# One plain chunk instead of two in each feed-forward block, and a pair opened among its matmuls

## The chip, the cores and the metric

The kernel runs on one core of a Trainium2 chip. The metric is the device time of one execution in microseconds (us), as the median of several runs. TensorE multiplies, VectorE and ScalarE work elementwise, GpSimd (POOL) does a few elementwise rows and issues the transfers that add to what is in SBUF, SyncE (SP) issues the loads.

## The reference

A trunk of two layers over two batches (512 and 256 tokens, width 1024). Each layer is `x += 1/2 SwiGLU(RMSNorm(x)); x += Mixer(RMSNorm(x)); x += 1/2 SwiGLU(RMSNorm(x))`, the mixers being a gated linear recurrence (layer 0) and windowed attention (layer 1). So there are four feed-forward blocks, here f0 to f3:

```python
def swiglu_ffn(x, w1, w2):               # w1: 1024 x 5632, w2: 2816 x 1024
    gate, up = jnp.split(x @ w1, 2, axis=-1)
    return (jax.nn.silu(gate) * up) @ w2
```

## The kernel before

**Split numbers.** Every operand is kept as a high half (a cast, on ScalarE) and a low half (what the cast left, a subtraction on VectorE), and a product is three matmuls: high by high, high by low, low by high. `split` does this for activations (L355 and L356), `quad_steps` for weights (L217 and L218).

**Seven products for eight.** The 768 tokens are two halves of 384, the 1024 inputs are two parts, and a chunk of 128 hidden units has a gate and an up column block. A *pair* (`up_pair`, matmuls on L549) makes the 2 x 2 x 2 blocks of one chunk by seven products p1 to p7 (Strassen's scheme in Winograd's form), each of four input tiles by three matmuls: 84 matmuls of 128x384. Each product has a weight factor (a11, a12, a21, a22 or sums of them) and an activation factor, by `FACTOR`: p1 takes b00 and p2 takes b10 (both of the first token half), p3 takes b11, and p7, p5, p6, p4 take the sums t3, t1, t2, t4 of all four blocks b00, b10, b01, b11. (In bRC, R is the input part and C the token half.) `sums` makes these four with subtractions and splits them.

**Plain chunks.** The sums need the second token half, which is normalised and transposed (`turn`, L421, L432) only while the block starts. So each block begins with `PLAIN` = 2 chunks without the scheme (`up_plain`, matmuls L350 to L352): 48 matmuls for a token half, 96 for a chunk. The other 20 chunks are pairs; after each four, `down_quad` multiplies by w2 in the same way.

**Weights.** `plan_ffn` lists the loads; `load_next` issues them on SP's queue into four raw buffers (`wr`), `take` and `ahead` stage their splits into eight buffers (`w`). For a pair, a partial tile `s` (L203) and a21 get their sums by transfers that add (`into`, L151, on POOL's queue). Two more sums, a11 += a21 ("second") and a12 += a11 ("fourth"), are additions on VectorE (L224), placed behind p5's and p4's split. p6 uses the first, p3 the second. p5's low half is made on POOL.

**Order.** A scheduler sets the order on each engine when the program is built, from the order in which the code is written; each engine then works through its own list in order. `later` and `run_later` put the second half's normalisation, transposes and sums between the plain chunks' matmuls.

Of the kernel before, what the change touches and what calls it, by code (L numbers as in the profile page):

```python
# [16 lines left out]
P = 128  # L17
D = 1024
DFF = 2816
NC = D // P  # L20
# [13 lines left out]
SEQS = ((0, TA), (TA, TB))  # L34
H = T // 2
HB = H // P
PLAIN = 2
GROUPS = (NF - PLAIN) // 4
WBUFS = 8
RAWBUFS = 4  # L40
# [14 lines left out]
class Trunk:  # L55
# [97 lines left out]
    def load_next(self):  # L153
        key, srcs, shape, how = self.queue.pop(0)
        if how in (TOK, OUT):
            self.loaded.append((len(srcs), self.tok_steps(key, srcs, how), 4))
            return
        raws = []
        for src in srcs:
            t = self.wp.tile([P, 1024], F32, tag="wr", name=self.name("wr"), bufs=RAWBUFS)  # L160
            raw = t[:, : shape[0] * shape[1]].rearrange("p (a b) -> p a b", a=shape[0])
            if len(srcs) < 4:
                src = src.rearrange("(k p) c -> p k c", p=P)
            self.last_load = self.nc.sync.dma_start(raw, src)
# [5 lines left out]
        free = 4  # L170
        if self.more.get(key):
            tail = self.tail_steps(key, self.more[key], how)
            steps = [step for both in zip(steps, tail) for step in both]
            free = 8
        self.loaded.append((len(raws), steps, free))

    def wtile(self):
        return self.wp.tile([P, 1024], F32R, tag="w", name=self.name("w"), bufs=WBUFS)
# [11 lines left out]
    def quad_steps(self, key, raws, srcs, order):  # L190
        nc = self.nc
        flat = lambda t: t.rearrange("p a b -> p (a b)")
        up = len(raws) == 2
        if up:
            a11, a12, a21, a22 = (flat(t[:, h : h + 4, :]) for t in raws for h in (0, 4))
            three = [srcs[1].rearrange("(k p) c -> p k c", p=P)[:, :4, :]]
        else:
            a11, a12, a21, a22 = (flat(t) for t in raws)
            three = [srcs[2][:, i : i + 1, :] for i in range(2)]
        s3 = []  # L200
        for i, src in enumerate(three):
            t = self.wp.tile([P, 512], F32, tag="s3", name=self.name("s3"), bufs=2)
            self.last_load = nc.sync.dma_start(t.rearrange("p (a b) -> p a b", a=src.shape[1]), src)  # L203
            self.into(t, a11[:, i * 512 : (i + 1) * 512])
            s3.append(t)
        self.into(a21, a22)

        def split(name, srcs, eng=None):
            if up:
                w = self.wtile()  # L210
                hi, lo = w[:, :512], w[:, 512:]
            else:
                hi, lo = self.wtile(), self.wtile()
            n = srcs[0].shape[-1]
            for i, src in enumerate(srcs):
                h, l = (t[:, i * n : (i + 1) * n] for t in (hi, lo))
                nc.scalar.copy(h, src)  # L217
                (eng or nc.vector).tensor_sub(l, src, h.bitcast(F32))  # L218
# [89 lines left out]
    def stage_next(self):  # L308
        if not self.loaded:
            self.load_next()  # L310
        steps = self.loaded[0][1]
        n, go = steps.pop(0)
        go()
        self.held += n
        if not steps:
            self.loaded.pop(0)
        inuse = lambda e: e[0] if len(e[1]) > e[2] or e[0] < 4 else 0
# [15 lines left out]
    def ahead(self):  # L333
        while self.queue or self.loaded:
            if not self.loaded:
                self.load_next()
            if self.held + self.loaded[0][1][0][0] > WBUFS:
                return
            self.stage_next()

# [132 lines left out]
        put("t2", b11)  # L473

    def sums(self):
        for kp in range(2):
            tiles = (self.tn[(i // 2, i % 2)][:, kp] for i in range(4))
            self.mix(*tiles, lambda name, src: self.put(name, kp, src))

    def spill_factors(self):  # L480
        self.kept = {}
# [22 lines left out]
            self.later(self.sums)  # L504

    def plan_ffn(self, tag, w1, w2):
        def up(i):
            gate, up = (w1[:, c * P : (c + 1) * P] for c in (i, NF + i))
            if i < PLAIN:
                self.plan((tag, i, 0), gate, (NC, P))  # L510
                self.plan((tag, i, 1), up, (NC, P))
            else:
                self.plan_quad((tag, i), (gate, up), (NC, P), UP)
# [12 lines left out]
    def up_plain(self, tag, j, half):  # L526
        pss = []
        for c in range(2):
            wh, wl = self.take((tag, j, c))
            ps = self.ps(H)  # L530
            for k in range(NC):
                b = self.operand(f"b{k // 4}{half}", k % 4)
                self.mm3(ps, (wh[:, k, :], wl[:, k, :]), b, k == 0, k == NC - 1)
                if half == 0 and k in (((), (2, 6)), ((3, 7), (3, 7)))[j][c]:
                    self.run_later()
            if half:
                self.done((tag, j, c))
            pss.append(ps)
        t = self.tmp(H)
# [19 lines left out]
    def up_pair(self, tag, j, opened=None):  # L559
# [29 lines left out]
        self.last_act = nc.scalar.activation(v, v, AF.Silu).ins  # L589
        self.last_dve = nc.vector.tensor_mul(w, v, w).ins  # L590
        yield w
        self.ahead()

    def down_quad(self, tag, g, hid):
# [82 lines left out]
    def ffn(self, tag, next_row):  # L677
        for g in range(GROUPS):
# [7 lines left out]
            def gather(ts, kp):  # L686
                self.mix(ts[0], ts[1], ts[2], ts[3], lambda name, src: put(name, src, kp))

            if g == 0:
                ts = {}  # L690
                for half in range(2):
                    for j in range(PLAIN):
                        t = ts[2 * j + half] = self.up_plain(tag, j, half)
                        name = f"b{j}{half}"
                        if name != "b01":
                            put(name, t, 0)
                gather(ts, 0)
                self.run_later(len(self.deferred))
            for kp in range(2):
                if g == 0 and kp == 0:  # L700
                    continue
                ts = []
                for j in range(2):
                    for half, t in enumerate(self.up_pair(tag, 4 * g + 2 * kp + j)):
                        ts.append(t)
# [925 lines left out]
```

## Time and profile before

| | |
|---|---|
| median of 3 runs | 2758.43 us (2758.16 to 2761.84) |
| profiled execution | 2759.27 us, span 2757.5 us |
| TensorE busy | 2736.1 us (99%) |
| VectorE busy | 2201.0 us (80%) |
| ScalarE busy | 1396.5 us (51%) |
| GpSimd busy | 460.7 us (17%) |
| granted TensorE clock | 0.999 |

In a row of a timeline the first number is the start in us from the span's start, the second how long the merged rows take from first start to last end, then engine, line, operation, what is written from what, shape and count; in brackets the idle time ahead and what ended it. In a row of groups the number behind the bar is the busy time, then the mean of one in ns. In a row of transfers the last number is the time from issue to landing. Matmuls overlap, so their starts tell more than their durations.

### The profile page before, as it was taken

What the parts mean: (1) busy time and instruction counts of PE and PEld (TensorE: products, weight loads), DVE (VectorE), ACT (ScalarE), POOL (GpSimd) and SP (SyncE); (2) the same over time, 40 slices, a digit from 0 to 9 for tenths busy, and PEclk for the clock granted to TensorE, in tenths of its full rate; (3) what the DMA queues carried; (4) which work ended last, traced back from release to release, by engine and by line L of the source; (5) the groups of instructions that cost most, each with busy time, mean ns of one, the idle gap of its engine ahead of it and who ended that gap; (6) DMA issues with size and microseconds to landing.
All of it is one profiled execution on the core that took longest, in us unless ns stands there. A gap on an engine that the chain in (4) does not pass through costs nothing. (4 is left out here: it accounts for less than half of the span.)

```text
span 2757.5 us, 40950 instructions
## 1 busy us (share of the span) xinstructions
PE 2736.1 (99%) x15081; PEld 2547.1 (92%) x15081; DVE 2201.0 (80%) x3766; ACT 1396.5 (51%) x2621; POOL 460.7 (17%) x507
## 2 busy tenths in 40 slices
PE   8999999999999999999999999999999999999998
PEld 8999999989999889999998999999888889999997
DVE  8788788767887888788878887887847868788877
ACT  6344444634455675444455543444458855444453
POOL 2111121200000101211120121112005611211120
PEclk9999999999999999999999999999999999999999
DMA  6554556751122743555454355545424422655453
GB/s 171 132 122 116 126 140 167 217 153 39 39 60 65 201 121 82 145 134 127 114 138 126 77 145 128 126 118 142 130 77 112 89 69 73 146 134 128 116 135 111
DMA packets 355048, 330.46 MB, mean 120 GB/s; under 512 B 14664, under 2 KB 271648, under 8 KB 354848
## 3 DMA queue, kind: packets, MB, share of 16 engines
q1 hardware_dynamic: 303744, 225.61, 27.6%
q0 software_dynamic: 46800, 88.76, 18.3%
q10 hardware_dynamic: 4304, 13.49, 1.4%
q8 instruction: 118, 1.93, 0.3%
q14 instruction: 82, 0.67, 0.1%
HBM read 226.87 MB, written 15.73 MB: 88 GB/s over the span
## 5 line engine op out<-in xcount | busy, mean ns | idle before, releaser
L549 PE MATMUL ps<-big,w 128*128 128x384 f32 x6720 | 1168.5, 334 | 0.0
L549 PEld LDWEIGHTS ps<-big,w 128*128 128x128 f32 x6720 | 1165.7, 188 | 1.4
L217 ACT CAST w<-wr 128x512 fp32r<-128x512 f32 x600 | 417.2, 706 | 651.6 <-PE ps L549 300.1
L218 DVE TENSOR_TENSOR w<-wr,w 128x512 fp32r<-128x512 f32 (+1 forms) x520 | 436.1, 842 | 138.1 <-ACT w L217 122.3
L615 PE MATMUL ps<-w,big 128*128 128x512 f32 x2016 | 460.7, 389 | 0.0
L615 PEld LDWEIGHTS ps<-w,big 128*128 128x128 f32 x2016 | 377.9, 188 | 78.8 <-DVE x L675 0.6
L151 POOL DMA_DIRECT2D s<-wr x126 | 110.5, 884 | 1220.7 <-DMA s<-in_ffn_w_dram 324.7
L675 DVE SCALAR_TENSOR_TENSOR x<-ps,x 128x512 f32<-128x512 f32 x420 | 272.7, 684 | 13.7 <-PE ps L647 13.1
L350 PE MATMUL ps<-big,w 128*128 128x384 f32 x640 | 219.2, 344 | 1.5 <-ACT w L184 1.0
L351 PE MATMUL ps<-big,w 128*128 128x384 f32 x640 | 215.1, 336 | 0.4 <-DVE big L356 0.3
L352 PE MATMUL ps<-big,w 128*128 128x384 f32 x640 | 214.5, 335 | 0.0
L355 ACT CAST big<-tA 128x384 fp32r<-128x384 f32 x308 | 153.6, 513 | 101.6 <-DVE tA L583 34.2
L356 DVE TENSOR_TENSOR big<-tA,big 128x384 fp32r<-128x384 f32 x308 | 176.3, 585 | 5.3 <-ACT big L355 3.4
L151 POOL DMA_DIRECT2D wr<-wr x109 | 95.3, 874 | 510.2 <-DMA wr<-in_ffn_w_dram 175.1
L831 PE MATMUL ps<-w,big 128*128 128x512 f32 x756 | 177.1, 392 | 0.1
L647 PE MATMUL ps<-w,big 128*128 128x512 f32 x756 | 174.5, 391 | 0.7 <-DVE x L675 0.6
L647 PEld LDWEIGHTS ps<-w,big 128*128 128x128 f32 x756 | 141.3, 188 | 30.5 <-DVE x L675 1.5
L831 PEld LDWEIGHTS ps<-w,big 128*128 128x128 f32 x756 | 140.5, 188 | 29.2 <-DVE w L356 0.6
L218 POOL TENSOR_TENSOR w<-wr,w 128x512 fp32r<-128x512 f32 x80 | 130.4, 1630 | 169.7 <-ACT w L217 152.6
L224 DVE TENSOR_TENSOR wr<-wr,wr 128x512 f32<-128x512 f32 (+1 forms) x120 | 123.6, 1030 | 20.4 <-issue 20.2
L350 PEld LDWEIGHTS ps<-big,w 128*128 128x128 f32 x640 | 120.1, 188 | 2.5 <-ACT w L184 1.3
L351 PEld LDWEIGHTS ps<-big,w 128*128 128x128 f32 x640 | 120.4, 188 | 1.4 <-DVE big L356 1.2
(219 smaller groups left out, 3647.3 us busy)
## 6 DMA issues: line engine op xcount, KB each, us to landing
wr<-in_ffn_w_dram SPq DMA_DIRECT2D x256, 512.0 KB, 4.0
s<-wr POOLq DMA_DIRECT2D x126, 256.0 KB, 4.5
s<-in_ffn_w_dram SPq DMA_DIRECT2D x120, 256.0 KB, 3.2
wr<-wr POOLq DMA_DIRECT2D x80, 256.0 KB, 3.9
wr<-in_hg_w_in_dram SPq DMA_DIRECT2D x32, 512.0 KB, 3.9
wr<-wr POOLq DMA_DIRECT2D x29, 512.0 KB, 4.6
spill<-x ACTq DMA_DIRECT2D x12, 512.0 KB, 3.9
kept<-big POOLq DMA_DIRECT2D x8, 768.0 KB, 7.9
```

Source lines behind the costliest of these rows:

```text
L151: self.nc.gpsimd.dma_start(out, src, accum_op=ALU.add)
L217: nc.scalar.copy(h, src)
L218: (eng or nc.vector).tensor_sub(l, src, h.bitcast(F32))
L350: nc.tensor.matmul(out, a[0], b[0], start=first, stop=False)
L351: nc.tensor.matmul(out, a[0], b[1], start=False, stop=False)
L352: nc.tensor.matmul(out, a[1], b[0], start=False, stop=last)
L356: self.nc.vector.tensor_sub(lo, src, hi.bitcast(F32))
L549: self.nc.tensor.matmul(ps, a[x], b[y], start=first and k == 0 and i == 0, stop=k == 3 and i == 2, skip_group_check=True,)
L615: nc.tensor.matmul(ps, a[x], w[y], start=name == chain and kp == 0 and q == 0, stop=kp == 1 and q == 2, skip_group_check=True,)
L647: nc.tensor.matmul(ps, a[x], w[y], start=name == chain and k == 0 and q == 0, stop=k == 2 and q == 2, skip_group_check=True,)
L675: self.nc.vector.scalar_tensor_tensor(x, ps, c, x, ALU.mult, ALU.add)
L831: nc.tensor.matmul(ps, x[:, sl], y, start=fresh and k == 0 and q == 0, stop=k == 3 and q == 2, skip_group_check=True,)
```

## The change

`PLAIN` becomes 1. Chunk 1 is a pair of a new form, `opened_pair`, whose p1 and p2 stand among the plain chunk's matmuls for the first token half (they need only b00 and b10). The rest of it follows the plain chunk's second token half, in the order p3, p7, p5, p6, p4. p3 gets a bank of its own. For this pair alone (`OPEN`) the "second" and "fourth" weight sums are made by adding transfers, behind p1's and p2's split, so p3's weight is there before p7's. `sums` goes factor by factor (t3, t1, t2, t4 with both input tiles) instead of input tile by input tile. Changes to `load_next` and `stage_next` only pass the count of buffers in another way.

```diff
-PLAIN = 2
+PLAIN = 1
 UP = ("p1", "p7", "p2", "p5", "p4", "p6", "p3")
+OPEN = ("p1", "p2", "p3", "p7", "p5", "p6", "p4")
...
+        if order == OPEN:
+            add = {"second": lambda: self.into(a11, a21), "fourth": lambda: self.into(a12, a11)}
+            behind, pin = {"p1": "second", "p2": "fourth"}, lambda ins: None
...
     def sums(self):
-        for kp in range(2):
-            tiles = (self.tn[(i // 2, i % 2)][:, kp] for i in range(4))
-            self.mix(*tiles, lambda name, src: self.put(name, kp, src))
+        sub = self.nc.vector.tensor_sub
+        b = lambda kp: [self.tn[(i // 2, i % 2)][:, kp] for i in range(4)]
+        for name, out, x, y in (("t3", 3, 1, 3), ("t1", 1, 0, 1), ("t2", 0, 0, 3), ("t4", 2, 2, 0)):
+            for kp in range(2):
+                t = b(kp)
+                sub(t[out], t[x], t[y])
+                self.put(name, kp, t[out])
...
+    def opened_pair(self, tag, j):
+        ...
+        p("p1", a, True, False)
+        nc.scalar.copy(v, a)
+        self.ahead()
+        yield
+        p("p2", a, False, True)
+        nc.scalar.activation(a, a, AF.Silu)
+        self.ahead()
+        yield
+        ...
+        p("p3", e, True, True)
+        nc.vector.tensor_add(u, v, e)
+        self.ahead()
+        p("p7", c, True, False)
+        nc.scalar.copy(w, c)
+        self.ahead()
+        p("p5", d, True, True)
+        nc.vector.tensor_sub(w, w, d)
+        nc.vector.tensor_add(u, u, d)
+        self.ahead()
+        p("p6", b, True, True)
+        nc.vector.tensor_sub(v, v, b)
+        nc.vector.tensor_sub(u, u, b)
+        nc.scalar.activation(u, u, AF.Silu)
+        nc.vector.tensor_sub(w, w, v)
+        nc.vector.tensor_mul(w, w, u)
+        yield 1, w
+        self.ahead()
+        p("p4", c, False, True)
+        nc.vector.tensor_sub(t, c, v)
+        nc.vector.tensor_mul(t, t, a)
+        yield 0, t
+        self.ahead()
...
             if g == 0:
-                ts = {}
-                for half in range(2):
-                    for j in range(PLAIN):
-                        t = ts[2 * j + half] = self.up_plain(tag, j, half)
...
+                first[PLAIN] = self.opened_pair(tag, PLAIN)
+                ts = {0: self.up_plain(tag, 0, first[PLAIN])}
+                self.run_later(2)
+                put("b00", ts[0], 0)
+                ts[1] = self.up_plain(tag, 1)
                 self.run_later(len(self.deferred))
```

Lines are numbered anew: L184 becomes L188, L217 and L218 become L221 and L222, L355 and L356 become L363 and L364, L432 becomes L440, L549 becomes L564.

On ScalarE in f0, the second token half before: the evictions of transposes for b01 and its casts, then at once those for b11 (big_331 is the transposed part, big_348 and big_351 the high halves of b11).

```order
34 L432 ACTIVATE big_278<-ps_274,cols 128x384
35 L432 ACTIVATE big_278<-ps_280,cols 128x384
36 L432 ACTIVATE big_278<-ps_285,cols 128x384
37 L432 ACTIVATE big_278<-ps_290,cols 128x384
38 L355 CAST big_295<-big_278 128x2x384
39 L355 CAST big_298<-big_278 128x2x384
40 L355 CAST big_307<-tA_304 128x384
41 L432 ACTIVATE big_331<-ps_327,cols 128x384
42 L432 ACTIVATE big_331<-ps_333,cols 128x384
43 L432 ACTIVATE big_331<-ps_338,cols 128x384
44 L432 ACTIVATE big_331<-ps_343,cols 128x384
45 L355 CAST big_348<-big_331 128x2x384
```

And now, from b01's casts on (w_255 is p3's weight, w_258 p7's, w_261 p5's, w_353 p6's):

```order
38 L363 CAST big_331<-big_314 128x2x384
39 L363 CAST big_334<-big_314 128x2x384
40 L221 CAST w_255<-wr_184 128x512
41 L221 CAST w_258<-s_35_188 128x512
42 L221 CAST w_261<-wr_186 128x512
43 L619 ACTIVATE ps_232<-ps_232 128x384
44 L221 CAST w_353<-wr_184 128x512
45 L440 ACTIVATE big_363<-ps_359,cols 128x384
46 L440 ACTIVATE big_363<-ps_365,cols 128x384
47 L440 ACTIVATE big_363<-ps_370,cols 128x384
48 L440 ACTIVATE big_363<-ps_375,cols 128x384
49 L363 CAST big_380<-big_363 128x2x384
```

Four weight casts, p3's first, have moved ahead of b11's evictions and casts. In f1, f2 and f3 p3's, p7's and p5's casts stand in the same way among or ahead of b01's evictions.

On POOL in f0 before: a21 += a22 and the partial tile of the first pair, the same two of the second, then p5's low half.

```order
8 L151 DMA wr_194<-wr_194 128x512
9 L151 DMA s_39_196<-wr_192 128x512
10 L151 DMA s_81_406<-wr_402 128x512
11 L151 DMA wr_404<-wr_404 128x512
12 L218 TENSOR_TENSOR w_500<-wr_194,w_500 128x512
```

And now: a21 += a22, the partial tile, a11 += a21, two adds of the next pair, a12 += a11, then p5's low half.

```order
8 L152 DMA wr_186<-wr_186 128x512
9 L152 DMA s_35_188<-wr_184 128x512
10 L152 DMA wr_184<-wr_186 128x512
11 L152 DMA wr_198<-wr_198 128x512
12 L152 DMA s_40_200<-wr_196 128x512
13 L152 DMA wr_184<-wr_184 128x512
14 L222 TENSOR_TENSOR w_261<-wr_186,w_261 128x512
```

Rows 10 and 13 have taken the place of VectorE's two additions, and row 13 ends the chain on which row 40 of ScalarE waits.

On VectorE in f0 now, from b11's low halves (big_380, big_383) to the next pair's first weight (w_457, its p1): L489 are the subtractions of the sums, L364 their low halves, t3 first and t4 last (big_411, big_415).

```order
46 L364 TENSOR_TENSOR big_380<-big_363,big_380 128x2x384
47 L364 TENSOR_TENSOR big_383<-big_363,big_383 128x2x384
48 L489 TENSOR_TENSOR big_363<-big_314,big_363 128x768 x2
...
58 L489 TENSOR_TENSOR big_295<-big_295,big_292 128x768 x2
59 L222 TENSOR_TENSOR w_446<-wr_186,w_446 128x512
60 L364 TENSOR_TENSOR big_411<-big_295,big_411 128x2x384
61 L364 TENSOR_TENSOR big_415<-big_295,big_415 128x2x384
62 L364 TENSOR_TENSOR big_418<-tA_356,big_418 128x384
63 L222 TENSOR_TENSOR w_457<-wr_196,w_457 128x512
```

The opened pair's p4 weight (w_446) and the next pair's p1 weight stand behind the sums. On TensorE 17 matmuls of that next pair (10 in f0) stand ahead of the opened pair's p4, two of its p1 with the high half alone.

More of the change, by code (lines that the diff above doesn't have):

```diff
@@ L169, in load_next @@
             steps = self.quad_steps(key, raws, srcs, how)
[L170 to L172 removed]
+        n, more = len(raws), self.more.get(key)
+        if more:
+            tail = self.tail_steps(key, more, how)
             steps = [step for both in zip(steps, tail) for step in both]
[L174 to L175 removed]
+        if n == 4:
+            inuse = lambda left: 4 if left > (8 if more else 4) else 0
+        else:
+            inuse = lambda left: n
+        self.loaded.append((steps, inuse))
     def wtile(self):
@@ L506, in plan_ffn, with halves @@
     def plan_ffn(self, tag, w1, w2):
+        def halves(i):
+            return [w1[:, c * P : (c + 1) * P] for c in (i, NF + i)]
         def up(i):
-            gate, up = (w1[:, c * P : (c + 1) * P] for c in (i, NF + i))
             if i < PLAIN:
-                self.plan((tag, i, 0), gate, (NC, P))
-                self.plan((tag, i, 1), up, (NC, P))
+                for c, w in enumerate(halves(i)):
+                    self.plan((tag, i, c), w, (NC, P))
             else:
-                self.plan_quad((tag, i), (gate, up), (NC, P), UP)
+                self.plan_quad((tag, i), halves(i), (NC, P), OPEN if i == PLAIN else UP)
         for g in range(GROUPS):
@@ L524, in plan_ffn, with up_plain @@
             self.plan_quad((tag, "down", g), srcs, (2, 512), LAST if last else DOWN, more)
-    def up_plain(self, tag, j, half):
+    def up_plain(self, tag, half, between=iter(())):
         pss = []
         for c in range(2):
-            wh, wl = self.take((tag, j, c))
+            wh, wl = self.take((tag, 0, c))
             ps = self.ps(H)
@@ L533, in up_plain @@
                 self.mm3(ps, (wh[:, k, :], wl[:, k, :]), b, k == 0, k == NC - 1)
-                if half == 0 and k in (((), (2, 6)), ((3, 7), (3, 7)))[j][c]:
+                if half == 0 and c and k in (2, 6):
                     self.run_later()
             if half:
-                self.done((tag, j, c))
+                self.done((tag, 0, c))
             pss.append(ps)
+            next(between, None)
         t = self.tmp(H)
@@ L591, in up_pair @@
         yield w
+        self.ahead()
+    def opened_pair(self, tag, j):
+        nc = self.nc
+        key = (tag, j)
+        a, v = self.ps(H), self.tmp(H)
+        p = lambda name, ps, first, last: self.product(key, name, FACTOR[name], ps, first, last)
+        p("p1", a, True, False)
[6 more added lines that the diff above has]
+        yield
+        b, c, d, e = (self.ps(H) for _ in range(4))
+        w, t, u = (self.tmp(H) for _ in range(3))
+        p("p3", e, True, True)
[20 more added lines that the diff above has]
+        yield 0, t
         self.ahead()
@@ L687, in gather @@
                 self.mix(ts[0], ts[1], ts[2], ts[3], lambda name, src: put(name, src, kp))
+            first = {}
             if g == 0:
-                ts = {}
-                for half in range(2):
-                    for j in range(PLAIN):
-                        t = ts[2 * j + half] = self.up_plain(tag, j, half)
[L694 to L697, printed above, removed]
+                first[PLAIN] = self.opened_pair(tag, PLAIN)
[3 more added lines that the diff above has]
+                ts[1] = self.up_plain(tag, 1)
                 self.run_later(len(self.deferred))
             for kp in range(2):
-                if g == 0 and kp == 0:
-                    continue
-                ts = []
+                if g or kp:
+                    ts = {}
                 for j in range(2):
-                    for half, t in enumerate(self.up_pair(tag, 4 * g + 2 * kp + j)):
-                        ts.append(t)
+                    i = 4 * g + 2 * kp + j
+                    if i < PLAIN:
+                        continue
+                    for half, t in first.get(i) or enumerate(self.up_pair(tag, i)):
+                        ts[2 * j + half] = t
                         name = f"b{j}{half}"
```

8 lines of the change are left out of this document (4 added, 4 removed).

## The prediction

> **What bounds the kernel now.** I read the page first (engines, groups), then TensorE's timeline at the start of each of the four feed-forward blocks (f0 to f3), then ScalarE and VectorE there, then the transfers.
>
> ```profile
> span 2757.5 us, 40950 instructions
> PE 2736.1 (99%) x15081; PEld 2547.1 (92%) x15081; DVE 2201.0 (80%) x3766; ACT 1396.5 (51%) x2621; POOL 460.7 (17%) x507
> ...
> L549 PE MATMUL ps<-big,w 128*128 128x384 f32 x6720 | 1168.5, 334 | 0.0
> ```
>
> TensorE is busy 2736.1 of 2757.5 us, so it bounds the kernel, and a removed matmul is worth what it holds the engine. That isn't the 334 ns of the group: the rows of one overlap the next.
>
> ```profile
> 30.39 0.33 PE L350 MATMUL ps<-big,w 128*128 128x384 f32 x1
> ...
> 43.39 0.33 PE L350 MATMUL ps<-big,w 128*128 128x384 f32 x1
> ...
> 52.23 8.08 PE L549 MATMUL ps<-big,w 128*128 128x384 f32 x45
> ...
> 1018.00 1.47 PE L421 MATMUL ps<-ident_r,big 128*128 128x128 f32 x12
> 1019.23 3.00 PE L831 MATMUL ps<-w,big 128*128 128x512 f32 x12
> ...
> 1060.55 5.71 PE L549 MATMUL ps<-big,w 128*128 128x384 f32 x32
> ...
> 1511.84 0.33 PE L350 MATMUL ps<-big,w 128*128 128x384 f32 x1
> ...
> 1548.04 4.15 PE L549 MATMUL ps<-big,w 128*128 128x384 f32 x23
> ...
> 2263.97 0.60 PE L350 MATMUL ps<-big,w 128*128 128x384 f32 x2
> ...
> 2300.73 3.45 PE L549 MATMUL ps<-big,w 128*128 128x384 f32 x19
> ```
>
> From 30.39 to 43.39 stand 25 triples (L350, L351, L352) without a gap: 75 matmuls in 13.00 us, 0.1733 us each. Twelve transposes take 1.23 (1018.00 to 1019.23). The L549 rows show where both plain chunks of f0, f1, f2 and f3 end and the pairs begin: 52.23, 1060.55, 1548.04, 2300.73. I compare those four ends with when the same two chunks are done after the change.
>
> **The change part by part.** *Fewer matmuls.* A plain chunk is 96 matmuls, a pair 7 products of 12, so each block loses 12, in all 48 x 0.1733 = 8.3 us if TensorE never waits. (By the group's 334 ns it would be 16 us, which is wrong.)
>
> *What takes its place.* 192 plain matmuls gave VectorE 33.3 us until the first sum (t3) was needed. Now it is needed after 72 + 48 + 12 = 132, 22.9 us. In that shorter time stand, per block, six splits of half a weight tile on VectorE and seven on ScalarE in place of two whole ones on each, and nine instead of two operations of the activation chain. So the two engines, which were hidden, come to the front.
>
> ```profile
> 28.50 1.58 ACT L355 CAST big<-big 128x768 fp32r<-128x768 f32 x2
> 29.96 0.53 ACT L355 CAST big<-tA 128x384 fp32r<-128x384 f32 x1
> 30.37 2.02 ACT L432 ACTIVATE big<-ps,cols 128x384 f32<-128x384 f32 x4
> 32.23 1.61 ACT L355 CAST big<-big 128x768 fp32r<-128x768 f32 x2
> ...
> 39.77 0.62 ACT L217 CAST w<-wr 128x512 fp32r<-128x512 f32 x1 [1.13 <-PE ps L351]
> 40.30 0.62 ACT L217 CAST w<-s 128x512 fp32r<-128x512 f32 x1
> ...
> 1028.35 1.60 ACT L355 CAST big<-big 128x768 fp32r<-128x768 f32 x2
> ...
> 1515.94 1.06 ACT L184 CAST w<-wr 128x1024 fp32r<-128x1024 f32 x1
> ```
>
> ```profile
> 33.34 1.83 DVE L356 TENSOR_TENSOR big<-big,big 128x768 fp32r<-128x768 f32 x2
> 35.08 1.82 DVE L458 TENSOR_TENSOR big<-big,big 128x768 f32<-128x768 f32 x2
> ...
> 46.83 0.70 DVE L218 TENSOR_TENSOR w<-wr,w 128x512 fp32r<-128x512 f32 x1
> 47.43 0.70 DVE L218 TENSOR_TENSOR w<-s,w 128x512 fp32r<-128x512 f32 x1
> ...
> 2263.77 1.82 DVE L356 TENSOR_TENSOR big<-big,big 128x768 fp32r<-128x768 f32 x2
> ```
>
> Start to start: a weight cast on ScalarE 0.53 (39.77 to 40.30), a pair of 768-wide casts 1.46 (28.50 to 29.96), four evictions of transposes 1.86 (30.37 to 32.23); on VectorE a 768-wide subtraction 0.87 (33.34 to 35.08 for two), a weight's low half 0.60 (46.83 to 47.43).
>
> *The new wait.* The weight of p3 is a12 + (a11 + (a21 + a22)), three adds by transfers on POOL's queue, each of which needs the one before and the second and third of which need p1's and p2's splits. ScalarE's order has the cast of p3 shortly behind p2's, and ahead of the second token half's evictions and casts (b01 and b11, or in f3 both). So ScalarE stands still until the third add has landed, and behind it stand b11, all four sums and TensorE.
>
> ```profile
> 10.69 8.90 SPq L164 DMA_DIRECT2D wr<-in_ffn_w_dram  x4
> ...
> wr<-in_ffn_w_dram SPq DMA_DIRECT2D x2, 512.0 KB, 9.8
> ...
> wr<-wr POOLq DMA_DIRECT2D x2, 256.0 KB, 3.9
> s<-wr POOLq DMA_DIRECT2D x2, 256.0 KB, 4.4
> ...
> DMA to landing us min/median/max: 3.3/4.8/5.7
> ...
> DMA to landing us min/median/max: 2.5/4.3/10.4
> ```
>
> The first row is SP's queue at the start, the second the weight loads issued at 11 to 12 us, the next two POOL's adds at 20 to 40 us, the last two all of POOL's transfers in 20 to 110 us and in the whole trace. No row shows three adds in a chain; I take 4.0 us for one, nearest to the 3.9 of this place, with 2.5 and 5.4 as bounds (5.7 seen once).
>
> When p3's third add lands:
> - f0: the chunk's second load is issued at about 11.1 and lands 9.8 later, 20.9. The partial tile behind it on SP's queue lands about 22 (estimate from those rows); its own add 4.8 later, 26.8, and a11 can't be overwritten before. Then 30.8 and 34.8. ScalarE is there at about 30.0, as before (29.96): 4.8 us idle.
> - f1: b10's casts end at 1029.8; p1's cast has replaced a longer one ahead (0.53 for 0.95), p2's ends at 1029.9, its low half behind b10's at 1031.1, landed 1035.1. ScalarE would be there about 3 us behind p2's cast (a copy, a table load, an activation and an eviction stand between), at 1033.
> - f2: ScalarE casts p2 at 1515.94, low half 1517.1, landed 1521.1; ScalarE would be there at 1519, by the same rows.
> - f3: p1's and p2's low halves follow b00's (2263.77 + 1.74 = 2265.5): 2266.1 and 2266.7. Both adds come late: 2270.1, 2274.1.
>
> From there to b11's low half: in f1 and f2 three casts, three evictions, two casts, four, two, and 0.9 on VectorE, 8.8 us; in f3 one eviction more, 9.3; in f0, where b01 is done already, 6.8. So b11 is ready at 41.6, 1043.9, 1529.9, 2283.4.
>
> Then VectorE alone: eight subtractions and eight low halves, 16 x 0.87 = 13.9, and, standing between, two weight splits and one or two 384-wide rows, 1.7 to 2.8. The last of these is the low half of the next pair's p1, which TensorE meets two matmuls into that pair. After it TensorE has 25 matmuls up to the end of p4, 17 of which belong to the next pair: both first chunks count as done 8 matmuls, 1.4 us, later. Ends: f0 41.6 + 15.6 + 1.4 = 58.6 (before 52.23, loses 6.4); f1 1043.9 + 16.2 + 1.4 = 1061.5 (loses 0.9); f2 1529.9 + 17.6 = 1547.5 (gains 0.5); f3 2283.4 + 16.7 + 1.4 = 2301.5 (loses 0.8). Sum: 7.6 us slower. The 8.3 us of matmuls are inside these ends.
>
> *Costed at nothing:* four added loads of 256 KB on SP, 16 added adds on POOL (those that aren't in the chain) and four more low halves on POOL, which is 17% busy. If POOL's low half of p5 came late, VectorE's sums, later still, would hide it. The order within sums() costs as much as before.
>
> The profiled execution took 2759.27 (its span 2757.5); the median of the runs is 2758.43, 0.84 lower. 2758.43 + 7.6 = 2766.0.
>
> **The rivals.**
> - *The adds land fast enough* (2.5 us each). For it: that has been seen; against it: the median is 4.3. Then f0's p3 is there at 29.5 and doesn't hold ScalarE: 30.0 + 6.8 + 15.6 + 1.4 = 53.8, loses 1.6. f1's lands at 1033.6: 1060.0, gains 0.5. f2 1519.6: 1546.0, gains 2.0. f3 2271.1: 2298.5, gains 2.2. In sum 3.1 faster, 2755.3. The Trainium skill, "DMA: Bandwidth & Descriptors", section "Anatomy of one DMA — SWDGE (gpsimd) path", speaks for it: a transfer issued by GpSimd is given there as about 2.0 us plus its bytes over 436 GB/s, which makes an estimate of 2.6 us for 256 KB and a time of 2755.7. This trace has only its fastest transfers there.
> - *Other side: nothing of the start is in the way.* The scheduler has put 17 matmuls of the next pair ahead of p4; if VectorE's and ScalarE's rows fall earlier than I place them (b11 by 1039 in f1), all 8.3 us are kept: 2750.1. It decides from when the next p1's low half is ready before TensorE gets to it, after 172 matmuls and 24 transposes, 32.3 us behind a block's start: 1544.1 in f2 (1511.84 + 32.3) and 2296.3 in f3 (2263.97 + 32.3), against my 1546.1 and 2300.1. Against it: f0, where VectorE has no gap before the sums.
> - *Slow adds* (5.4 each): f0's chain lands at 38.2, 3.4 later, f1 and f2 1.4, f3 2.8. 9 us more than forecast: 2775.
>
> **How the numbers follow.** Less than 0.2% (5.5 us) can't be told from no change. Forecast 0.45 and slow adds 0.13, both slower: 0.58. Fast adds 0.29: same. Nothing in the way 0.13: faster. The range, 2753 to 2775, reaches from a little under the fast adds' 2755.3 to the slow adds' 2775 and leaves out the case with nothing in the way and what lies beyond the slow adds. The likeliest one's own range is 2761 to 2771.
>
> **What would show it.** ScalarE idle ahead of a weight cast and released by POOL's transfer, about 5, 2, 2 and 4 us at the four starts; VectorE without gaps from b11 to the next pair's weights; TensorE idle at the end of the opened pair, in f0 most (both near 36 to 40 us and near 54 to 57 us); 48 matmuls fewer. It is wrong if ScalarE reaches p3 later than the add, or if TensorE shows no more idle time than before at the four starts.

## The result, and the profile after

The changed kernel takes 2783.36 us (median of 4 runs, 2782.13 to 2784.11) against 2758.43 before: a ratio of 1.0087, 95% interval 1.007 to 1.0105. It is slower, as forecast, but by 25 us where 7.6 were forecast, and outside the range. The head of the page of after, and its costliest group:

```profile
span 2782.3 us, 41006 instructions
PE 2737.3 (98%) x15033; PEld 2543.5 (91%) x15033; DVE 2216.6 (80%) x3810; ACT 1405.5 (51%) x2647; POOL 490.5 (18%) x527
...
L564 PE MATMUL ps<-big,w 128*128 128x384 f32 x7056 | 1236.2, 335 | 14.0 <-DVE w L222 8.9
```

TensorE has 48 matmuls fewer (15033 for 15081) and yet is busy 1.2 us longer (2737.3 for 2736.1), so part of what is left runs slower; and the pairs' matmuls, which had no idle time before them, now have 14.0 us. TensorE's waits in the whole trace of after (us in all, times, the longest) name most of it:

```profile
PE ps L564 <- DVE w L222: 8.9, 4, 3.6
...
PE ps L358 <- ACT big L363: 7.0, 2, 6.8
PE ps L669 <- DVE x L729: 3.7, 3, 1.7
PE ps L564 <- ACT tA L581: 2.2, 1, 2.2
```

The four waits of 8.9 us are one in each feed-forward block: the next pair's first weight, which VectorE hands over too late, as forecast. The 6.8 us are f0's stop for b11. The other two rows, in the first w2 product and in the next pairs, stand in no step of the prediction. TensorE's timeline of after shows them in order, f0 first:

```profile
33.87 0.34 PE L358 MATMUL ps<-big,w 128*128 128x384 f32 x1
41.04 0.69 PE L358 MATMUL ps<-big,w 128*128 128x384 f32 x1 [6.83 <-ACT big L363]
41.52 0.52 PE L359 MATMUL ps<-big,w 128*128 128x384 f32 x1
41.84 0.52 PE L360 MATMUL ps<-big,w 128*128 128x384 f32 x1
...
60.40 15.75 PE L564 MATMUL ps<-big,w 128*128 128x384 f32 x80 [3.61 <-DVE w L222]
76.63 16.94 PE L564 MATMUL ps<-big,w 128*128 128x384 f32 x96 [0.47 <-DVE tA L592]
93.40 4.28 PE L669 MATMUL ps<-w,big 128*128 128x512 f32 x18
99.40 12.98 PE L669 MATMUL ps<-w,big 128*128 128x512 f32 x56 [1.71 <-DVE x L729]
...
1074.10 32.94 PE L564 MATMUL ps<-big,w 128*128 128x384 f32 x176 [2.02 <-DVE w L222]
1106.88 4.96 PE L669 MATMUL ps<-w,big 128*128 128x512 f32 x21
...
1565.40 16.09 PE L564 MATMUL ps<-big,w 128*128 128x384 f32 x90 [1.69 <-DVE w L222]
1582.02 15.34 PE L564 MATMUL ps<-big,w 128*128 128x384 f32 x86 [0.53 <-DVE tA L592]
1597.20 4.96 PE L669 MATMUL ps<-w,big 128*128 128x512 f32 x21
...
2321.02 9.11 PE L564 MATMUL ps<-big,w 128*128 128x384 f32 x51 [1.57 <-DVE w L222]
2332.32 22.30 PE L564 MATMUL ps<-big,w 128*128 128x384 f32 x125 [2.18 <-ACT tA L581]
```

Three things are to be seen. First the stops in brackets. Second the pace: after the stop at 41.04 the matmuls start 0.32 us apart instead of 0.1733, and in f1 176 matmuls take 32.8 us (1074.10 to 1106.88) where 176 x 0.1733 is 30.5. Third the tail: a second stop a few matmuls into the w2 product (L669). That product began, before the change, at these places of TensorE's timeline:

```profile
81.47 17.88 PE L615 MATMUL ps<-w,big 128*128 128x512 f32 x78
...
1577.15 23.10 PE L615 MATMUL ps<-w,big 128*128 128x512 f32 x101
```

It ran there without a stop, 78 and 101 matmuls in one row (all 126 of the product took 28.6 us in each block). Taking as a block's end the first matmul of its last w2 product (458.06 before and 471.98 after in f0, and so on through both traces), the blocks lose 13.9, 4.4, 2.75 and 4.0 us, f0 to f3. Between the blocks the distance changes by less than 0.4 us. These marks carry some noise: in the run with the order of the sums alone, which takes as long as the kernel before, they move by up to 0.5 us a block.

The engines behind it, in f0. ScalarE's p3 cast (L221) with its idle time; VectorE's b11 low halves, a stretch of the sums, and the next pair's p1 low half (L222); POOL's adds and p5's low half:

```profile
35.81 0.62 ACT L221 CAST w<-wr 128x512 fp32r<-128x512 f32 x1 [6.86 <-DMA wr<-wr]
```

```profile
37.67 1.75 DVE L654 TENSOR_TENSOR x<-x 128x512 f32<-128x512 f32 x1
...
41.02 1.83 DVE L364 TENSOR_TENSOR big<-big,big 128x768 fp32r<-128x768 f32 x2 [0.39 <-ACT big L363]
42.76 2.69 DVE L489 TENSOR_TENSOR big<-big,big 128x768 f32<-128x768 f32 x3
...
48.80 3.80 DVE L489 TENSOR_TENSOR big<-big,big 128x768 f32<-128x768 f32 x3
...
59.67 0.68 DVE L222 TENSOR_TENSOR w<-wr,w 128x512 fp32r<-128x512 f32 x1
```

```profile
27.92 1.77 POOL L152 DMA_DIRECT2D wr<-wr  x2 [5.80 <-DMA s<-wr]
29.00 1.59 POOL L152 DMA_DIRECT2D s<-wr  x1
31.85 0.85 POOL L152 DMA_DIRECT2D wr<-wr  x1 [1.27 <-DMA wr<-wr]
37.55 1.32 POOL L222 TENSOR_TENSOR w<-wr,w 128x512 fp32r<-128x512 f32 x1 [4.85 <-ACT w L221]
...
50.36 1.42 POOL L222 TENSOR_TENSOR w<-wr,w 128x512 fp32r<-128x512 f32 x1 [4.76 <-ACT w L221]
```

The forecast chain is there: adds issued at 27.92 and 31.85, p3's cast at 35.81 after 6.86 us of idle ScalarE, b11 at 42.8, the next pair's first weight at 60.35. What is open is how much of 25 us hangs on the adds, how much on VectorE's own work, and what the pace costs.

### The profile page after: what moved, and what is told of

It is laid out like the page before. It is cut to its first block, busy times and chain, and to the rows that moved or that the text cites. A ratio compares the mean times of both kernels' runs of the same rounds, so it can differ in the third digit from the quotient of the medians.

```text
span 2782.3 us, 41006 instructions
## 1 busy us (share of the span) xinstructions
PE 2737.3 (98%) x15033; PEld 2543.5 (91%) x15033; DVE 2216.6 (80%) x3810; ACT 1405.5 (51%) x2647; POOL 490.5 (18%) x527
## 5 line engine op out<-in xcount | busy, mean ns | idle before, releaser
L564 PE MATMUL ps<-big,w 128*128 128x384 f32 x7056 | 1236.2, 335 | 14.0 <-DVE w L222 8.9
L564 PEld LDWEIGHTS ps<-big,w 128*128 128x128 f32 x7056 | 1227.0, 188 | 20.1 <-DVE w L222 10.2
L221 ACT CAST w<-wr 128x512 fp32r<-128x512 f32 (+1 forms) x624 | 431.7, 703 | 669.4 <-PE ps L564 274.3
L222 DVE TENSOR_TENSOR w<-wr,w 128x512 fp32r<-128x512 f32 (+1 forms) x540 | 442.3, 822 | 151.6 <-ACT w L221 141.5
L669 PE MATMUL ps<-w,big 128*128 128x512 f32 x2016 | 461.4, 390 | 3.8 <-DVE x L729 3.7
L669 PEld LDWEIGHTS ps<-w,big 128*128 128x128 f32 x2016 | 377.8, 188 | 83.3 <-DVE x L729 3.4
L729 DVE SCALAR_TENSOR_TENSOR x<-ps,x 128x512 f32<-128x512 f32 x420 | 272.3, 683 | 13.2 <-PE ps L701 12.7
L363 ACT CAST big<-tA 128x384 fp32r<-128x384 f32 x308 | 153.7, 513 | 111.0 <-DVE tA L598 31.7
L152 POOL DMA_DIRECT2D wr<-wr x121 | 106.3, 882 | 561.0 <-DVE w L222 191.6
L364 DVE TENSOR_TENSOR big<-tA,big 128x384 fp32r<-128x384 f32 x308 | 179.1, 594 | 7.1 <-ACT big L363 5.6
L358 PE MATMUL ps<-big,w 128*128 128x384 f32 x512 | 177.8, 348 | 7.0 <-ACT big L363 7.0
L359 PE MATMUL ps<-big,w 128*128 128x384 f32 x512 | 172.8, 338 | 1.2 <-DVE big L364 1.0
L360 PE MATMUL ps<-big,w 128*128 128x384 f32 x512 | 171.8, 336 | 0.0
L222 POOL TENSOR_TENSOR w<-wr,w 128x512 fp32r<-128x512 f32 x84 | 143.4, 1707 | 130.9 <-ACT w L221 130.9
L592 DVE TENSOR_TENSOR tA<-tA,ps 128x384 f32<-128x384 f32 x80 | 44.0, 550 | 82.7 <-PE ps L564 82.7
L358 PEld LDWEIGHTS ps<-big,w 128*128 128x128 f32 x512 | 96.9, 190 | 7.8 <-ACT big L363 7.6
```

Source lines behind the costliest of these rows:

```text
L152: self.nc.gpsimd.dma_start(out, src, accum_op=ALU.add)
L358: nc.tensor.matmul(out, a[0], b[0], start=first, stop=False)
L359: nc.tensor.matmul(out, a[0], b[1], start=False, stop=False)
L360: nc.tensor.matmul(out, a[1], b[0], start=False, stop=last)
L364: self.nc.vector.tensor_sub(lo, src, hi.bitcast(F32))
L564: self.nc.tensor.matmul(ps, a[x], b[y], start=first and k == 0 and i == 0, stop=k == 3 and i == 2, skip_group_check=True,)
```

## The experiments

Two theories. W: the wait for the adding transfers, ahead of p3's cast, is what costs. S: VectorE and ScalarE have too little time under the shorter cover, with or without transfers. All runs are compared with the kernel before on the same chip (medians 2757.6 to 2758.1 there). What a run brings against the change is the difference of the two medians, though the chips differ by up to 0.8 us. The losses by block are taken at the marks named above, in the one profiled execution of each run.

**The weight sums on VectorE.**

```diff
         if order == OPEN:
-            add = {"second": lambda: self.into(a11, a21), "fourth": lambda: self.into(a12, a11)}
             behind, pin = {"p1": "second", "p2": "fourth"}, lambda ins: None
```

> The changed kernel, but the opened pair's two weight sums (a11 += a21 and a12 += a11) are additions on VectorE again, at the place where the change has the adding transfers, so p3's weight waits for no transfer that follows p2's split. If the transfers' wait is what costs (theory W): ScalarE's idle time of 6.9 us ahead of p3's cast in the first block f0 goes nearly away, b11's low halves end near 37 us instead of 42.8, and most of the 11.9 us that f0 lost comes back: 2771 to 2775 us. If VectorE and ScalarE simply have too little time under the shorter cover (theory S), two more additions on VectorE per block (about 0.7 us each) make it as slow or slower: 2783 to 2788 us.

2777.67 us, ratio 1.007 (1.0056 to 1.0084): 5.7 us better than the change, between the two theories. The blocks lose 10.0, 4.8, 1.4 and 2.5. ScalarE's wait ahead of p3's cast is gone, but in f0 VectorE now stands still for 4.1 us ahead of the first addition, with the second half's normalisation queued behind it. The row names no releaser; the partial tile's add, which reads a11 before the addition may overwrite it, was issued at 21.68 and landed 6.1 us later, at 27.8 (a21 + a22 was there at 26.5). TensorE meets that at the transposes, and ScalarE stands 5.2 us behind it. VectorE's and TensorE's timelines of this run:

```profile
27.89 0.69 DVE L228 TENSOR_TENSOR wr<-wr,wr 128x512 f32<-128x512 f32 x1 [4.14 <-issue]
```

```profile
29.30 2.03 PE L428 MATMUL ps<-ident_r,big 128*128 128x128 f32 x10 [3.80 <-DVE big L410]
```

**Without the two weight sums.** (a21 + a22 and the partial tile are still made by transfers.)

```diff
-            add = {"second": lambda: self.into(a11, a21), "fourth": lambda: self.into(a12, a11)}
+            add = {"second": lambda: None, "fourth": lambda: None}
```

> The changed kernel with the opened pair's two weight sums left out altogether (p6 and p3 of that pair take a11 and a12 as they were loaded), on no engine and on no queue. It is the lower bound of what the wait for the sums costs. W: f0's loss falls from 11.9 to about 3 us, f1 to f3 gain 0 to 2 us each: 2768 to 2773 us. S: within 4 us of the changed kernel, 2779 to 2784 us.

2770.66, ratio 1.0046 (1.0033 to 1.0058). So the wait for the sums is worth 12.7 us, in every block (they now lose 8.1, 1.9, 0.6 and 1.6). That is half of the loss; 12.6 us stay above the kernel before on this chip, and S has to answer for them or something else. In f0 ScalarE still waits 2.9 us here, for the partial tile's add ahead of p7's cast.

**p3's cast behind b11's.**

```diff
-OPEN = ("p1", "p2", "p3", "p7", "p5", "p6", "p4")
+OPEN = ("p1", "p2", "p7", "p5", "p3", "p6", "p4")
...
+    def extra(self, steps):
+        return 3 if steps and steps[0][1] in self.late else 0
...
-            if self.held + self.loaded[0][0][0][0] > WBUFS:
+            n = self.loaded[0][0][0][0]
+            if self.held + n + self.extra(self.loaded[0][0]) > WBUFS:
                 return
```

(`late` holds p3's step; the products stand in the same new order.)

> The changed kernel with all its transfers, but p3's weight is staged only when the plain chunk's first weight is done with, so that its cast stands behind b11's evictions and casts on ScalarE instead of ahead of them, and the opened pair's products go p7, p5, p3, p6, p4. The number and duration of the instructions are the same, only the order differs. W: the idle time of ScalarE ahead of b11 goes (6.9 us in f0, 1.4 in f1), the sums begin some 5 us earlier in f0: 2770 to 2775 us. S: 2781 to 2786 us, since the same work fills the same engines.

2792.03, ratio 1.0126 (1.0112 to 1.014): both theories missed, it is 8.7 us slower than the change (the profiled execution took 2796.2). b11's low halves do end 3.3 us earlier in f0 (39.5). But p3's and p6's splits now come behind the sums on VectorE, and until then they hold the raw buffer of a11 and a12, so SP's loads for the third pair begin at 57.56 instead of 40.05, and ScalarE stands still again, ahead of the cast of that pair's partial tile, with the opened pair's activation rows behind. SP's queue and ScalarE's timeline of this run:

```profile
57.56 1.03 SPq L166 DMA_DIRECT2D wr<-in_ffn_w_dram  x2
```

```profile
68.52 0.62 ACT L222 CAST w<-s 128x512 fp32r<-128x512 f32 x1 [4.17 <-DMA s<-wr]
```

A wait that is taken from one queue came back in another, through the four raw buffers.

**The order of the sums alone** (the kernel before with the new `sums()`).

> The kernel before with nothing but the new sums(): t3, t1, t2, t4 by factor instead of by input tile. The prediction costed the order at nothing. If so: 2757 to 2760 us. A rival is that the order of the sums itself makes the first pair's p7 or p5 late: then some 2 us per block, 2764 to 2768 us.

2758.11, ratio 1.0 (0.9992 to 1.0009). The order costs nothing, as the prediction had it.

**Spare matmuls in the stop.**

```diff
+        if j == PLAIN + 1:
+            wh, b0 = self.take((*key, "p1"))[0], self.operand("b00", 0)[0]
+            for _ in range({"f0": 18, "f1": 10}.get(tag, 0)):
+                nc.tensor.matmul(a, wh[:, 0, :], b0, start=True, stop=True, skip_group_check=True)
         p("p1", a, True, False)
```

> The changed kernel with idle TensorE time filled: ahead of the next pair's p1, where TensorE waits for that weight's low half, 18 spare matmuls in f0 (3.1 us) and 10 in f1 (1.7 us) into the pair's own bank, which p1 then overwrites. The wait itself stays (3.6 and 2.0 us). In the changed kernel the 176 matmuls behind this wait take some 2 us more than 176 x 0.1733 in f0 and in f1. Theory 'slow pace after a stop': the spare matmuls keep the pace, the time falls by 3 to 4.5 us, to 2779 to 2780.5 us. Rival: the lost time behind the wait is late weights and factors, not the pace: 2783 to 2785 us.

2778.99, ratio 1.0076 (1.0064 to 1.0089): 4.4 us less than the change, with more work done, at the edge of the expected interval. Two stretches of f0, in order: us, TensorE busy, weight loads, VectorE, ScalarE, POOL, then the granted clock, the transfers' share and GB/s. In the changed kernel:

```profile
58.00:62.00 4.00, 1.60 (x9) 1.60 (x10) 4.00 (x8) 0.59 (x2) 0.00 (x0) 0.98 0.45 131
62.00:66.00 4.00, 4.00 (x16) 4.00 (x15) 4.00 (x9) 1.80 (x3) 0.90 (x1) 0.59 0.81 171
```

and with the spare matmuls:

```profile
58.00:62.00 4.00, 3.70 (x22) 3.39 (x21) 4.00 (x8) 1.69 (x4) 0.00 (x0) 1.00 0.44 131
62.00:66.00 4.00, 4.00 (x25) 4.00 (x24) 4.00 (x9) 1.13 (x2) 0.90 (x1) 1.00 0.58 130
```

With TensorE idle from 56.8 to 60.4, the granted clock falls to 0.59 in the next stretch and 16 matmuls fit in 4 us; kept busy, it stays at 1.00 and 25 fit. So this stop is paid twice, once as idle time and once as slow pace behind it. Not all of the 4.4 us is the price of the pace: the slow matmuls that went are worth about 1.6 us in f0 and as much in f1, f1 got a stop of 1.09 us among its next pairs, and the first w2 products take 1.7, 1.0 and 0.8 us less in f0 to f2, though f2 has no spare matmuls. Nor does every stop have a slow stretch behind it: the 4 us of the changed kernel in which f3's stop of 2.18 us ends show the full clock.

```profile
2332.00:2336.00 4.00, 3.69 (x21) 3.69 (x22) 3.29 (x6) 2.57 (x6) 1.25 (x1) 1.00 0.37 65
```

The Trainium skill, "TensorE: Matmul & The Clock Gate", section "Part 1: The HAM clock gate (the "warmup" mystery)", says that the array's clock is halved after an idle window of about 3.4 us and freed after a busy one. The trace agrees with the halving (0.32 us for 0.1733, granted clock 0.50 from 62 to 65 us), but f1's stop of 2.02 us was enough for it, while f0's of 0.8 us at 19 us and f3's of 2.18 us were not; the length of a stop alone doesn't tell here.

**The next pair's low halves on POOL.**

```diff
+LOWS = ("p1", "p7", "p2")
...
-            split(name, own[name], nc.gpsimd if up and name == "p5" else None)
+            split(name, own[name], nc.gpsimd if up and (name == "p5" or key[1] == PLAIN + 1 and name in LOWS) else None)
```

> The changed kernel, but the low halves of the next pair's p1, p7 and p2 weights are made on POOL (as p5's is), so TensorE no longer waits for VectorE to get behind all sums before it can begin that pair. The prediction's formula says that this row of VectorE sets the end of the first two chunks. If so, the waits for it (3.6, 2.0, 1.7 and 1.6 us in f0 to f3) and the slow pace behind them go: 2769 to 2774 us. Rival: VectorE's backlog only shows at the next thing that TensorE needs from it (the sums t4 and t1, p4's weight, the pair's later factors), or POOL's rows are too slow beside a busy VectorE: 2779 to 2786 us.

2797.47, ratio 1.0145 (1.013 to 1.0161): 14 us worse than the change, beyond the rival too. In f2, POOL's first such row took 10.70 us beside VectorE's sums, and the next ones stretched VectorE's rows from 0.69 to 1.77. POOL's, VectorE's and TensorE's timelines of this run:

```profile
1559.42 10.70 POOL L223 TENSOR_TENSOR w<-wr,w 128x512 fp32r<-128x512 f32 x1
1570.09 1.28 POOL L223 TENSOR_TENSOR w<-s,w 128x512 fp32r<-128x512 f32 x1
```

```profile
1566.09 0.69 DVE L223 TENSOR_TENSOR w<-wr,w 128x512 fp32r<-128x512 f32 x1
...
1570.15 1.77 DVE L229 TENSOR_TENSOR wr<-wr,wr 128x512 f32<-128x512 f32 x1 [0.23 <-POOL w L223]
1571.84 1.77 DVE L223 TENSOR_TENSOR w<-wr,w 128x512 fp32r<-128x512 f32 x1
```

```profile
1570.17 9.83 PE L565 MATMUL ps<-big,w 128*128 128x384 f32 x55 [2.53 <-POOL w L223]
```

The two engines hinder each other row by row, so POOL is no relief for a full VectorE. The Trainium skill, "SBUF — State Buffer", section "SBUF: two separate sides", has the rule: a port pair shared by VectorE and GpSimd is locked for a whole instruction, and two-tensor rows of VectorE ask for it against a GpSimd row that reads SBUF. These rows fit it.

**x's rows later.**

```diff
-            for i in range(HB):
-                x12, x21, x22 = cols(HB + i, 0), cols(i, 1), cols(HB + i, 1)
-                nc.vector.tensor_add(x12, x12, x22)
-                nc.vector.tensor_sub(x21, x21, x22)
+            with self.tc.issue_after(self.mark):
+                for i in range(HB):
+                    x12, x21, x22 = cols(HB + i, 0), cols(i, 1), cols(HB + i, 1)
+                    nc.vector.tensor_add(x12, x12, x22)
+                    nc.vector.tensor_sub(x21, x21, x22)
```

(`mark` is the next pair's last row on VectorE.)

> The changed kernel, but the six 512-wide rows per block that prepare x for the first w2 product stand behind the next pair on VectorE; in the changed kernel some of them stand ahead of b11's low halves and of the sums (four of them in f0, 2.4 us). If the time of VectorE's own rows is what bounds the start of the blocks (theory S): about 2 us less per block, 2773 to 2778 us. If ScalarE's wait for the transfers sets when b11 is there (theory W; in f0 VectorE waits 0.4 us for b11's cast): 2780 to 2784 us.

2788.73, ratio 1.0112 (1.0099 to 1.0126): 5.4 us slower than the change, neither theory's number. f0 gains 0.6, as W said. f1 loses 3.9 more; there the scheduler also placed p1's matmuls otherwise (8.5 us behind the block's start instead of 1.3), so that the run doesn't test one thing alone. I leave it open.

**f0 as before, the change in f1 to f3** (`plan_ffn`, `up_plain` and `ffn` take two plain chunks where the tag is f0).

> The change in f1, f2 and f3 only; f0 keeps its two plain chunks and the adds on VectorE, with sums() by factor everywhere. By the marks in the two traces f0 loses 13.9 us and the other three 4.4, 2.7 and 4.0. If the blocks' losses add up: 2758.4 + 11.1 = 2769.5 us (2768 to 2771). If a part of f0's loss only moves (a queue or buffers that f0 leaves in another state): over 2773 us.

2770.78, ratio 1.0047 (1.0034 to 1.0059): the blocks' losses add up within 1.5 us (f1 to f3 lose 5.4, 3.75 and 3.3), and half of the 25 us is f0's.

**t4 late.**

```diff
-    def sums(self):
+    def sums(self, which=("t3", "t1", "t2")):
...
+            if name not in which:
+                continue
...
         yield 1, w
         self.ahead()
+        self.sums(("t4",))
         p("p4", c, False, True)
```

> The changed kernel, but the fourth sum (t4: two subtractions and two low halves on VectorE, 4 x 0.87 = 3.5 us) is made only behind the next pair's p1, p7 and p2 weights and part of the opened pair's activation rows; TensorE runs the next pair's p1, p7, p5 and p6 before the opened pair's p4. So the next pair's p1 low half is ready 3.5 us earlier. If VectorE's queue up to this row is what TensorE waits for: the waits of 3.6, 2.0, 1.7 and 1.6 us go, and the slow pace behind them (about 4.5 us): 2769 to 2774 us. Rival: VectorE's backlog is as long as before and TensorE meets it a few rows later (as with the low halves on POOL): 2779 us or more.

2778.53, ratio 1.0076 (1.0063 to 1.0088): 4.8 us better than the change, of 9 to 14 expected. In f1 to f3 the wait for the first weight went (they lose 3.5, 1.5 and 1.0). In f0 it went too, to 0.16 us, but nothing was gained: TensorE stopped 1.8 and 1.9 us for t4 instead, in its timeline

```profile
58.01 8.62 PE L566 MATMUL ps<-big,w 128*128 128x384 f32 x48 [0.16 <-DVE w L222]
68.43 0.44 PE L566 MATMUL ps<-big,w 128*128 128x384 f32 x1 [1.80 <-ACT big L363]
70.78 23.76 PE L566 MATMUL ps<-big,w 128*128 128x384 f32 x127 [1.91 <-DVE big L364]
```

So in f0 it was VectorE's backlog, of which the first weight was only the first sign.

**t4 late, and the sums on VectorE.**

> The t4-late order together with the opened pair's two weight sums as additions on VectorE (which alone brought 5.7 us). If the wait for the adds and the length of VectorE's queue are separate losses: 2764 to 2768 us. If they overlap: 2768 to 2773 us. If it all only moves: 2777 us.

2773.42, ratio 1.0055 (1.0041 to 1.0069). Alone the two edits bring 4.8 and 5.7 us, together 9.9, so they are nearly separate savings; the time that I expected for that was missed because t4 late brings less than I had expected of it.

**f0 as before, f1 to f3 with both edits.**

> f0 as before with its two plain chunks; f1, f2 and f3 opened, with t4 late and the weight sums on VectorE. With VectorE's additions f1 to f3 lost 4.8, 1.4 and 2.5 us; if the waits for the next pair's first weight and the slow pace go there too (some 8 us), the rest is about even with the kernel before: 2757 to 2762 us. A gain of 6.2 us (36 matmuls fewer) would show only with no wait left at all: 2752 us. Rival, backlog: 2765 to 2768 us.

2761.04, ratio 1.0011 (1.0002 to 1.002): as expected about even with the kernel before, not better. The first w2 product takes 1.4, 1.1 and 1.2 us longer in f1 to f3 than in the kernel before, which eats what the pairs gain in f2 and f3 (the blocks lose 1.7, 0.05 and 0.2). Its second stop in f1 of this run:

```profile
1095.38 19.79 PE L674 MATMUL ps<-w,big 128*128 128x512 f32 x86 [1.09 <-DVE x L734]
```

**Fewer rows on VectorE** (the low halves of t1, t2 and t4 are left out).

```diff
-                self.put(name, kp, t[out])
+                if full or name == "t3":
+                    self.put(name, kp, t[out])
+                    continue
+                o = self.big([P, 2, 2, H], F32R)
+                self.nc.scalar.copy(o[:, :, 0, :], t[out])
+                self.ops[(name, kp)] = HighOnly(o)
```

> The changed kernel with less work on VectorE: at the start of the four feed-forward blocks the low halves of t1, t2 and t4 are left out (the high half stands in for them), six rows of 0.87 us, 5.2 us per block. If the length of VectorE's queue is what is left of the loss once the wait for the adds is set aside: TensorE's waits for the next pair's first weight (8.9 us in all), the slow pace behind them (some 4 us) and part of the waits in the first w2 product go: 2766 to 2771 us. Rival, the rest is made by transfers and raw buffers that come free late: 2777 us or more.

2767.9, ratio 1.0035 (1.0023 to 1.0047): 15.5 us better than the change, and all four waits for the first weight are gone. f1 to f3 lose 0.9, -1.4 and -1.2; f0 still loses 12.5, with the stop for the adds (6.6 us) in place.

**Both away.**

> Both taken away: no weight sums in the opened pair (as in the run that brought 12.7 us) and no low halves of t1, t2 and t4. If the wait for the adds and VectorE's queue together are the cause, the 48 matmuls that the change removes (8.3 us) begin to show: 2752 to 2757 us, below the kernel before. If something else costs as well, such as TensorE's stop ahead of b11 in f0: 2757 to 2761 us. If there is a third cause of the same size: 2765 us or more.

2756.87, ratio 0.9997 (0.9988 to 1.0006). That is 26.5 us less than the change, and in f2 and f3 all that the change removes shows at last: 228 matmuls without a stop, and blocks that end 2.5 and 2.3 us earlier than before (f1 2.0; 12 matmuls are 2.08). TensorE's timeline of this run:

```profile
1538.09 39.68 PE L578 MATMUL ps<-big,w 128*128 128x384 f32 x228
...
2288.04 39.68 PE L578 MATMUL ps<-big,w 128*128 128x384 f32 x228
2327.56 17.66 PE L683 MATMUL ps<-w,big 128*128 128x512 f32 x77
```

Only f0 still loses 4.5 us, with stops of 0.7 and 1.9 us ahead of b01 and 1.7 in the first w2 product. The first two follow from the add that is left: ScalarE waits 2.9 us for the partial tile at p7's cast, with b01's evictions behind it. Alone the two edits bring 12.7 and 15.5 us, together 26.5. The wait for the adds (12.7 us) and VectorE's rows (13.8 us on top of it) are thus shown as the two causes; the slow pace is how part of both is paid (about 1.6 us behind each of two stops).

## Why the prediction was wrong in size

- *Mechanism and direction*: right. ScalarE waits for POOL's adds (6.9, 1.4, 0.6 and 3.5 us in f0 to f3, where about 5, 2, 2 and 4 were forecast), b11 is late, VectorE runs through the sums, and TensorE stops for the next pair's first weight.
- *The price of an add*, 4.0 us: right for f0. The second and third add of f0 were issued 3.9 us apart (27.92, 31.85) and the cast began 4.0 after the third; in f1 the cast began 3.3 after it (1045.51, 1048.84). The rival with fast adds fell. The estimate of 2.6 us from the Trainium skill, "DMA: Bandwidth & Descriptors", section "Anatomy of one DMA — SWDGE (gpsimd) path", is not what this place shows either. p3's cast came at 35.81 for 34.8, since the first adds were 1.1 us later than the estimate; in f1 it came at 1048.84, and 1035.1 plus the 13.56 us by which the block began later is 1048.7.
- *The step that failed first: f0's stretch from b11 to the first weight*, 15.6 us predicted, 17.5 measured (42.8 to 60.35). The rows were right (0.87 us each), but one sum row lasted 1.1 longer beside POOL's low half at 50.36 (3.80 for three instead of 2.69), and VectorE had a gap of 0.7. With the later adds f0 came 3.1 us later than forecast there; f1, f2 and f3 0.35, 1.0 and 0.
- *The term that was missing: the pace behind a stop.* The prediction multiplied every matmul by 0.1733. Behind the stops the changed kernel's matmuls took longer by 1.9, 2.3, 0.6 and 0.6 us, worked out from their starts in its timeline. The halved clock is about 1.6 us of it in f0 and as much in f1 (some ten matmuls 0.32 us apart). The rest, and all of f2's and f3's (granted clock 1.00), are single matmuls that started 0.2 to 0.3 us after the one before; what held them up is left open.
- *"Costed at nothing": what follows the opened pair.* VectorE's backlog was not over with the first weight. TensorE stopped again in the next pairs (0.5, 0.5 and 2.2 us in f0, f2 and f3) and in the first w2 product, which took 2.0, 1.1, 1.5 and 0.45 us longer.
- *The sum*: 7.6, and 4.4 for the later first weights, 5.4 for the pace and the single late matmuls, 3.2 for the second stops and 5.0 for the w2 product, make 25.6; by its mark, f2 regains 0.5 later in the block, which leaves 25.1. The prediction ended its account of a block at the first two chunks; the last two terms, more than two fifths of what it missed, lie behind that point.
- *The rival on the other side*, that all 8.3 us are kept, holds in no run as a whole. Only with both loads taken away do f1 to f3 keep their share (6.8 us, where 36 matmuls are 6.2).
- *The costs taken as nothing that held*: the order of the sums.

## What to carry to other kernels

Work that TensorE is spared also shortens the cover of the engines that feed it; count what those engines must do until the *last* place where TensorE catches up with them, not until the first. A stop of TensorE can cost more than its idle time: behind some of the stops here the granted clock was halved for about 3 us. And when a wait is moved, look for the buffers that the moved instruction now holds longer.

## What the runs showed of the hardware

- After f1's stop of 2.02 us and f0's of 3.61 us the granted clock of a 4 us stretch behind them fell to about 0.6; after f3's of 2.18 us it stayed at 1.00. In the run without the two weight sums TensorE resumed at 34.16, after 1.92 us of idle time and 0.64 us shortly before, at its full pace, and only from 35.48 to 38.7 its matmuls started 0.32 us apart: the slow stretch comes with a delay, and costs there 1.6 us beside the stop's 1.92. The ends of it in TensorE's timeline of that run:

```profile
34.16 0.44 PE L359 MATMUL ps<-big,w 128*128 128x384 f32 x1 [1.92 <-DVE big L364]
...
35.48 0.52 PE L360 MATMUL ps<-big,w 128*128 128x384 f32 x1
...
38.68 0.43 PE L360 MATMUL ps<-big,w 128*128 128x384 f32 x1
```

- One 512-wide row of VectorE took 1.75 us instead of 0.69 beside a POOL row (37.67 and 37.55 above), and POOL's rows of that size took 1.3 to 13.5 us (the longest in f1 of the run with three low halves more on POOL; in the changed kernel the longest took 10.4 us, in f1): neither engine's mean duration holds where the other is full.
